# A gated trunk layer with three token mixers: a value head computed in the idle half of the key tile, longer modulation dots, and the norm's scale kept in PSUM

## The chip, the cores and the metric

The kernel runs on one core of one Trainium2 chip. The metric is the time of one execution in microseconds of device time. Three runs of the kernel before the change took 1243.07 to 1245.12 us, median 1244.29.

## The reference

Two layers over 512 tokens of width 1024, in float32. What matters here, cut from the reference:

```python
mod = c_silu @ w_ada + b_ada                       # one vector per layer
shift, scale, gate = jnp.split(mod, 3, axis=-1)
u = rms_norm(x, norm_g) * (1 + scale[:, None]) + shift[:, None]
z = u @ w_in
(aq, ak, av, ag, iq, ik, iw, bq, bk, bv, bg, cq, ck, cv, cg, ma, mb, mc) = jnp.split(z, SPLIT_OFFSETS, axis=-1)
...
merged = (jax.nn.sigmoid(ma) * (ya @ w_br_a) + jax.nn.sigmoid(mb) * (yb @ w_br_b) + jax.nn.sigmoid(mc) * (yc @ w_br_c))
return x + gate[:, None] * (merged @ w_out)
```

ya, yb and yc are the outputs of a sparse attention with an indexer, a sliding-window attention with two key and value heads (bv has 128 columns, 64 per head), and a stick-breaking attention. The indexer has one key of 64 columns (ik), to which the rotary embedding is applied. After the second layer there is a last rms norm.

## The kernel before, in words

**Data.** Activations lie transposed: 128 features on the partitions, 512 tokens along the free axis, eight such tiles for a width of 1024. A float32 product is made of three matmuls: each operand is split into a rounded high part and a remainder (uh and ul for u, whi and wlo for a weight), and high x high, low x high and high x low are added up in PSUM. Weights arrive in chunks of 128 x 512 (tile wstage) and are split on ACT, DVE or POOL.

**Stages of a layer.** `first_phase` (L880) computes the seven tiles of `FIRST` (L57) k step by k step, as each u tile becomes ready: two gate tiles (cg0, cg1), two merge gates (mc0, mc1), the indexer's key (ik) and its queries (iq0, iq1). The key has 64 columns only, so its tile holds it twice. Seven accumulators take all three ps_z slots and four of the five ps_s slots. `v_phase` (L929) computes what is wanted with tokens on the partitions, the values and the indexer's weights: here u is the stationary operand, and 1156 weight columns (`VCOLS`) stream in three groups of 386, 386 and 384 (`VGRP`, L75), for 8 k steps and 4 token blocks each. Then come the three mixers, gates and branch products, interleaved, and `out_phase` (L1291), which adds the result to x, sums the squares for the next norm and, in the last layer, writes the result.

**Norm and modulation.** The sum of squares comes from a matmul with a matrix of -1 into a PSUM bank (`nbank`); `rstd_of` (L748) takes Ln and Exp on ACT, from PSUM into an SBUF tile `zs`. `make_u` (L752) multiplies x by the norm's gain times (1 + scale) (`amul`, one number per partition) and by rstd in one DVE instruction, adds the shift (ACT), rounds to uh and subtracts for ul. For the first two tiles shift and rounding are one step.

The modulation vector is a product of a vector with a matrix. It is computed on DVE as dots of a 128 x 512 piece of weights with the broadcast vector (`csr`), with an accumulator output; two pieces make one column of `mods`. In layer 0 the dots for shift and scale stand in the way of the first u tiles: `ada_load` (L706) and `ada_first` (L711), four pieces of 256 KB for each k step, staged in the slots of tiles yh and yl that the mixers use later. Their elementwise result goes to another tile (`junk`, L686). For the first k step some filler matmuls (`FILL`, L42) read the staged pieces. The dots of later modulations run in other stages, on other tiles.

**Rotary.** `rope_evac` (L791) copies the tile from PSUM to zs, moves 32-row blocks by four DMAs into m2, multiplies by cosine and sine tables and adds.

**Order of the work.** The functions only record instructions. `Weave` interleaves the stages' items, and `Recorder` (L244 on) then plans: each instruction has a modelled price (`price`, L304), may run on one of several engines where alternatives are given, and each tile class has a fixed number of slots (`SLOTS`, L150). `forward` (L372) schedules all instructions by these prices, five rounds with priorities taken from the round before, and the best round's order is emitted for each engine. In the model a DMA lands 1.9 us after its issue, or when the DMA before it has landed, plus its bytes over 290 GB/s (L316, L460). All engines run in order, so a changed price can move any instruction of the program. All instructions have line L536 in the profile, so groups go by tiles.

Of the kernel before, what the change touches and what calls it, by code (L numbers as in the profile page):

```python
# [25 lines left out]
F32 = mybir.dt.float32  # L26
F32R = mybir.dt.float32r
# [25 lines left out]
def _cols(name, lo, n):  # L53
# [7 lines left out]
    ("mc1", _cols("mc", 128, 128)),  # L61
    ("ik", _cols("ik", 0, 64) + _cols("ik", 0, 64)),
    ("iq0", _cols("iq", 0, 128)),
# [12 lines left out]
VOFF = (0, 386, 772)  # L76

# [44 lines left out]
def by_tile(wv, *gens):  # L122
# [6 lines left out]
    while live:  # L129
# [15 lines left out]
        else:  # L145
# [3 lines left out]

SLOTS = {"t": 14, "e": 2, "zs": 2, "m2": 2, "zc": 2, "G": 2, "sm": 2, "yh": 5, "yl": 5, "Q": 2, "KH": 2, "dot": 2, "dotg": 2,  # L150
         "m8": 2, "mx": 2, "nm": 2, "den": 2, "wstage": 4, "whi": 4, "wlo": 4, "ps_z": 3, "ps_s": 5}
# [92 lines left out]
class Recorder:  # L244
# [59 lines left out]
    def price(self, x, engine, op, args, kw):  # L304
# [254 lines left out]
def trunk(ctx, tc, xT, vecs, w_ss, w_gt, w_first, w_t, w_v, w_br, w_o, rope, consts, out):  # L559
# [125 lines left out]

    def junk(l, m, w):  # L686
        if l == 0 and m < 16:
            return t512("t", 10) if m % 8 < 2 else t512("e", 2)
        return w

    def dot(l, m, q, w, o):
        DVE.scalar_tensor_tensor(junk(l, m, w), w, 1.0, csr[:, S * (q % 2):S * (q % 2) + S], op0=OP.mult, op1=OP.mult, accum_out=o[:, q:q + 1])
        if q % 2:
            DVE.tensor_scalar(mods[l][:, m:m + 1], o[:, q - 1:q], o[:, q:q + 1], b_ada[l][:, m:m + 1], op0=OP.add, op1=OP.add)
# [11 lines left out]
    def ada_load(j):  # L706
        st["wada", j] = [t512(t, 5) for t in ("yh", "yl", "yh", "yl")]
        for q in range(4):
            SP.dma_start(st["wada", j][q], w_ss[0, j, q])

    def ada_first(j):  # L711
        for q in range(4):
            if j < 2:
                for _ in range(FILL[4 * j + q]):
                    mm(st["nbank" if j else "warm"][:, :P], f(nones), st["wada", j][q][:, :P], not j)
            ada_step(0, j, q, st["wada", j][q])

# [22 lines left out]
    def rstd(cs_):  # L740
        if cs_.start == 0:
            st["nbank"], st["rstd"] = sbank(), t512("zs", 2)
        p, t = st["nbank"][:, cs_], st["rstd"][:, cs_]
        mm(p, f(nones), st["sq"][:, cs_], True, False)
        mm(p, f(nones), st["sq7"], False)
        rstd_of(p, t)

    def rstd_of(p, t):  # L748
        ACT.activation(t, p, AF.Ln, bias=epst, scale=-1.0 / D)
        ACT.activation(t, t, AF.Exp, scale=-0.5)  # L750

    def make_u(l, k, xk, cs_=FULL):  # L752
        t = t512("e", 2)[:, cs_]
        sh = mods[l][:, k:k + 1]
# [4 lines left out]
        uh, ul = st["uh"][k][:, cs_], st["ul"][k][:, cs_]  # L759
        if k < 2:  # L760
            if l == 0 and (k or cs_.start):
                ACT.activation(uh, t, AF.Identity, bias=sh)
            else:
                DVE.tensor_scalar(uh, t, sh, None, op0=OP.add)
            DVE.scalar_tensor_tensor(ul, t, sh, f(uh), op0=OP.add, op1=OP.subtract)
        else:
            ACT.activation(t, t, AF.Identity, bias=sh)
            cast(uh, t)
            both(ul, t, f(uh), OP.subtract)

# [63 lines left out]
    def evac(name, z):  # L834
        kind = name[:2] if name[2:] else name
        if kind in ("ag", "bg", "cg"):
            gate_evac(z, name)
        elif kind in ("ma", "mb", "mc"):
            m_evac(z, name)
        elif kind == "cq":  # L840
            st[name] = stack_q(z, 0.125, sbuf=False)
        elif kind == "ck":
            st[name] = stack_k(z, sbuf=False)
        elif kind in ("aq", "bq", "iq"):
            st[name] = stack_q(rope_evac(z))
# [34 lines left out]
    def first_phase(l):  # L880
# [29 lines left out]
        if l == 0:  # L910
            yield op(0, lambda: ada_load(3))
            yield op(0, lambda: ada_first(2))
        yield op(0, lambda: make_u(l, 2, st["x"][2]))
        yield op(9000, two if l else two0, *chunks(0), *chunks(1))
        for k in range(2, KT):
            if k + 1 < KT:
                if l == 0:
                    if k + 2 < KT:
                        yield op(0, lambda k=k: ada_load(k + 2))
                    yield op(0, lambda k=k: ada_first(k + 1))  # L920
                yield op(0, lambda k=k: make_u(l, k + 1, st["x"][k + 1]))

# [6 lines left out]
    def v_phase(l):  # L929
        def prep():  # L930
            st["vc"] = rec.tile("vc", [P, 4, S], F32)
            st["va"] = rec.tile("va", [P, 4, S], F32)
            st["vb"] = rec.tile("vb", [P, 4, P], F32)
            st["iw"] = rec.tile("iw", [P, 4, 4], F32)
        yield op(0, prep)
        dests = (("vc", 0, 512, 1.0), ("vb", 512, 640, 1.0), ("va", 640, 1152, 1.0), ("iw", 1152, 1156, 0.0625))
        for g in range(3):
# [353 lines left out]
    def out_phase(l):  # L1291
# [74 lines left out]
    def start():  # L1366
# [17 lines left out]
        x = st["x"] = [xx[k // 4][:, k % 4] for k in range(KT)]  # L1384
        nb = st["nbank"] = sbank()
        st["rstd"] = t512("zs", 2)

        def norm(cs_):
# [3 lines left out]
            for k in range(0, KT, 2):  # L1392
# [141 lines left out]
```

## Time and profile before

| | |
|---|---|
| median of three runs | 1244.29 us |
| the profiled execution | 1245.02 us |
| its span, first to last instruction | 1243.2 us |
| first tiles of layer 0, first to last matmul | 13.7 to 65.6 us |
| value stage of layer 0 | 65.6 to 116.1 us |
| first tiles of layer 1, value stage of layer 1 | 629 to 669 us, 669 to 716 us |
| last matmul of the output product | about 1233.5 us |

PE is TensorE, PEld its weight loads, DVE VectorE, ACT ScalarE, POOL GpSimd, and SP the engine that issues most DMAs. An instruction is named by its tiles, out<-in: `ps_z<-uh,whi` is a matmul into a PSUM tile of class ps_z. Ends of matmuls are modelled, so the spacing of starts, not the length of a row, tells the rate.

### The profile page before, as it was taken

The page shows a single profiled execution, that of the slowest core. Times are in us where ns is not written, and L with a number is a line of the kernel's source. Part 1 is how long each engine was busy: PE and PEld are TensorE (multiplying, and loading weights), DVE is VectorE, ACT ScalarE, POOL GpSimd, SP SyncE. Part 2 cuts the span into 40 slices and gives each one's busy share as a digit, 9 for nine tenths or more (in the row PEclk, how much of TensorE's full clock was granted, in tenths as well). Part 3 has the DMA queues.
Part 4 walks back from the last instruction along what each step waited for, and adds up shares of the span by engine and source line. Part 5 has one row for each costly group of instructions (what it writes and reads, how often), then busy time and mean ns, then how long its engine had stood idle before and what let it go on. Part 6 is the DMA issues. An engine that isn't in the chain of part 4 may idle for free.

```text
span 1243.2 us, 17837 instructions
## 1 busy us (share of the span) xinstructions
PE 1212.5 (98%) x5976; PEld 986.7 (79%) x5976; DVE 977.9 (79%) x2152; ACT 560.0 (45%) x1157; POOL 242.6 (20%) x274
## 2 busy tenths in 40 slices
PE   7899999999999999999999999999999999999997
PEld 5699777778877887778899987777787788877886
DVE  7966999999778877777476589999886888667654
ACT  4343677553255532642143157764533554244212
POOL 1010334532122111011200015343310211100120
PEclk9999999999999999999999999999999999999999
DMA  9644232324433455334633422223342233322243
GB/s 315 202 123 125 77 94 58 96 93 134 113 102 94 136 155 143 93 119 119 191 106 97 132 88 85 77 77 102 102 127 68 77 102 110 102 69 77 93 119 102
DMA packets 82012, 139.67 MB, mean 112 GB/s; under 512 B 10240, under 2 KB 22784, under 8 KB 81920
## 3 DMA queue, kind: packets, MB, share of 16 engines
q1 hardware_dynamic: 80768, 136.44, 36.8%
q10 hardware_dynamic: 1152, 2.10, 0.5%
q8 instruction: 47, 0.77, 0.3%
q14 instruction: 45, 0.37, 0.1%
HBM read 125.91 MB, written 4.19 MB: 105 GB/s over the span
## 4 chain that ended last, share of the span: by engine, by line
PE 80%; DVE 12%; ACT 3%; DMA 2%; issue 1%; SPq 1%; DVEq 0%; ACTq 0%
PE ps_z L536 58%; PE ps_s L536 22%; DVE t L536 4%; DVE Q L536 2%; SPq L536 1%; DVE m L536 1%; ACT t L536 1%; DVE e L536 1%; DVE score L536 1%; DVE vc L536 1%; DMA m<-zs 1%; DVE wstage L536 1%; DVE wlo L536 1%; DMA yl<-in_w_ss 0%; DMA wstage<-in_w_t 0%
## 5 line engine op out<-in xcount | busy, mean ns | idle before, releaser
L536 PE MATMUL ps_z<-uh,whi 128*128 128x512 f32 (+1 forms) x908 | 359.8, 398 | 7.6 <-ACT uh L536 4.9
L536 PE MATMUL ps_z<-ul,whi 128*128 128x512 f32 (+1 forms) x908 | 356.5, 393 | 0.0
L536 PE MATMUL ps_z<-uh,wlo 128*128 128x512 f32 (+1 forms) x908 | 355.4, 392 | 0.0
L536 POOL TENSOR_TENSOR wlo<-wstage,whi 128x512 fp32r<-128x512 f32 (+1 forms) x129 | 170.4, 1322 | 677.8 <-DVE whi L536 365.6
L536 PEld LDWEIGHTS ps_z<-uh,whi 128*128 128x128 f32 x908 | 170.8, 189 | 48.5 <-ACT uh L536 6.5
L536 PEld LDWEIGHTS ps_z<-uh,wlo 128*128 128x128 f32 x908 | 171.0, 188 | 38.5 <-issue 0.3
L536 PEld LDWEIGHTS ps_z<-ul,whi 128*128 128x128 f32 x908 | 171.3, 189 | 37.4 <-issue 2.6
L536 DVE CAST whi<-wstage 128x512 fp32r<-128x512 f32 (+2 forms) x181 | 76.3, 422 | 128.6 <-PE ps_z L536 109.8
L536 DVE TENSOR_TENSOR wlo<-wstage,whi 128x512 fp32r<-128x512 f32 (+2 forms) x243 | 159.2, 660 | 16.1 <-ACT whi L536 7.7
L536 ACT CAST whi<-wstage 128x512 fp32r<-128x512 f32 (+2 forms) x138 | 81.5, 596 | 168.1 <-PE ps_z L536 115.9
L536 ACT ACTIVATE e<-ps_z 128x512 f32<-128x512 f32 x68 | 40.3, 593 | 125.6 <-PE ps_z L536 125.4
L536 ACT ACTIVATE e<-e 128x512 f32<-128x512 f32 x96 | 60.3, 631 | 47.2 <-DVE e L536 46.3
L536 ACT ACTIVATE t<-t,nm 128x256 f32<-128x256 f32 (+3 forms) x128 | 65.1, 510 | 29.1 <-DVE nm L536 29.1
L536 ACT ACTIVATE t<-t 128x512 f32<-128x512 f32 x120 | 72.5, 628 | 7.3 <-DVE t L536 4.1
L536 PE MATMUL ps_z<-yh,wlo 128*128 128x512 f32 x192 | 75.8, 395 | 0.0
L536 PE MATMUL ps_z<-yl,whi 128*128 128x512 f32 x192 | 75.7, 394 | 0.0
L536 PE MATMUL ps_z<-yh,whi 128*128 128x512 f32 x192 | 75.7, 396 | 0.0
L536 PE MATMUL ps_s<-small,t 128*128 128x128 f32 x432 | 59.7, 276 | 4.8 <-ACT t L536 3.8
L536 PEld LDWEIGHTS ps_s<-small,t 128*128 128x128 f32 x432 | 49.4, 141 | 16.8 <-ACT t L536 6.0
L536 POOL CAST whi<-wstage 128x512 fp32r<-128x512 f32 (+1 forms) x53 | 33.3, 628 | 129.7 <-PE ps_z L536 98.4
L536 DVE MAX8 m<-score 128x8 f32<-128x256 f32 (+2 forms) x96 | 53.3, 555 | 1.4
L536 DVE SCALAR_TENSOR_TENSOR wstage<-wstage,csr 128x512 f32<-128x512 f32 x64 | 46.4, 725 | 7.4 <-DMA wstage<-in_w_ss 5.5
(202 smaller groups left out, 2164.5 us busy)
## 6 DMA issues: line engine op xcount, KB each, us to landing
wstage<-in_w_t SPq DMA_DIRECT2D x212, 256.0 KB, 2.7
m<-zs SPq DMA_DIRECT2D x128, 64.0 KB, 2.0
wstage<-in_w_gt SPq DMA_DIRECT2D x32, 256.0 KB, 2.6
wstage<-in_w_ss SPq DMA_DIRECT2D x32, 256.0 KB, 2.7
wstage<-in_w_o SPq DMA_DIRECT2D x32, 256.0 KB, 2.6
wstage<-in_w_v SPq DMA_DIRECT2D x32, 193.0 KB, 2.5
yh<-in_w_ss SPq DMA_DIRECT2D x16, 256.0 KB, 5.1
yl<-in_w_ss SPq DMA_DIRECT2D x16, 256.0 KB, 5.2
```

Of the source, the lines that this page charges most:

```text
L536: getattr(self.real[engine], y.op)(*[real(a) for a in y.args], **{k: real(v) for k, v in y.kw.items()})
```

## The change

Six things, in one diff:

1. The second half of the ik tile holds the 64 columns of the second value head of bv. `key_and_value` copies the tile to zs, builds the key's second half by a DMA, applies rotary, and brings the value half to tokens on the partitions by four transposes into a ps_s bank and a copy. The value stage then streams 1092 columns in three groups of 364.
2. The dots of layer 0 take 1024 columns each, staged in one class `Y` of 128 x 1024 tiles by DMAs of 512 KB, and overwrite their weights in place. The bias is added by a TENSOR_TENSOR.
3. rstd stays in PSUM: Ln and Exp write the bank of the sum of squares.
4. x is multiplied by rstd in place (`times_rstd`), on DVE, as soon as rstd is there.
5. `make_u` then computes scale and shift in one instruction, twice: once rounded (uh) and once not (t), each on ACT or DVE, and ul is their difference.
6. The planner's DMA rate is 365 GB/s instead of 290.

```diff
-    ("ik", _cols("ik", 0, 64) + _cols("ik", 0, 64)),
+    ("ik", _cols("ik", 0, 64) + _cols("bv", 64, 64)),
...
-VCOLS = _cols("cv", 0, 512) + _cols("bv", 0, 128) + _cols("av", 0, 512) + _cols("iw", 0, 4)
-VGRP = (386, 386, 384)
+VCOLS = _cols("cv", 0, 512) + _cols("bv", 0, 64) + _cols("av", 0, 512) + _cols("iw", 0, 4)
+VGRP = (364, 364, 364)
...
-            y.cost, y.lag, y.mode = 0.35 if engine == "SP" else 0.1, n * 4 / 290e3, "dma"
+            y.cost, y.lag, y.mode = 0.35 if engine == "SP" else 0.1, n * 4 / 365e3, "dma"
...
     def ada_load(j):
-        st["wada", j] = [t512(t, 5) for t in ("yh", "yl", "yh", "yl")]
-        for q in range(4):
-            SP.dma_start(st["wada", j][q], w_ss[0, j, q])
+        st["wada", j] = [rec.tile("Y", [P, 2 * S], F32) for _ in range(2)]
+        for i in range(2):
+            SP.dma_start(st["wada", j][i].rearrange("p (a b) -> p a b", a=2), w_ss[0, j, 2 * i:2 * i + 2].rearrange("q p s -> p q s"))
     def ada_first(j):
...
+        o = rec.tile("dot", [P, 4], F32)
+        for i in range(2):
+            w, m = st["wada", j][i], 8 * i + j
             if j < 2:
...
+                for q in range(2):
+                    for _ in range(FILL[4 * j + 2 * i + q]):
+                        mm(st["nbank" if j else "warm"][:, :P], f(nones), w[:, S * q:S * q + P], not j)
+            DVE.scalar_tensor_tensor(w, w, 1.0, csr, op0=OP.mult, op1=OP.mult, accum_out=o[:, i:i + 1])
+            DVE.tensor_tensor(out=mods[0][:, m:m + 1], in0=o[:, i:i + 1], in1=b_ada[0][:, m:m + 1], op=OP.add)
+        DVE.scalar_tensor_tensor(amul[0][:, j:j + 1], mods[0][:, 8 + j:9 + j], 1.0, g_sb[0][:, j:j + 1], op0=OP.add, op1=OP.mult)
...
+    def rstd_of(t):
+        ACT.activation(t, t, AF.Ln, bias=epst, scale=-1.0 / D)
         ACT.activation(t, t, AF.Exp, scale=-0.5)
+    def times_rstd(xk, cs_=FULL):
+        DVE.tensor_tensor(out=xk[:, cs_], in0=xk[:, cs_], in1=st["rstd"][:, cs_], op=OP.mult)
     def make_u(l, k, xk, cs_=FULL):
         t = t512("e", 2)[:, cs_]
-        DVE.scalar_tensor_tensor(t, xk[:, cs_], amul[l][:, k:k + 1], st["rstd"][:, cs_], op0=OP.mult, op1=OP.mult)
+        sc, sh = amul[l][:, k:k + 1], mods[l][:, k:k + 1]
...
+        for o in (st["uh"][k][:, cs_], t):
+            rec.add({"ACT": ("activation", (o, xk[:, cs_], AF.Identity), dict(scale=sc, bias=sh)),
+                     "DVE": ("tensor_scalar", (o, xk[:, cs_], sc, sh), dict(op0=OP.mult, op1=OP.add))})
+        both(st["ul"][k][:, cs_], t, f(st["uh"][k][:, cs_]), OP.subtract)
...
+    def key_and_value(z):
+        zs, m2, zc = t512("zs"), t512("m2"), t512("zc")
+        cast(zs, z)
+        cast(zc[H0], z[H0])
+        SP.dma_start(zc[H1], zs[H0])
+        for a, b in ((0, 32), (32, 0), (64, 32), (96, 0)):
+            SP.dma_start(m2[a:a + 32], zs[b:b + 32])
+        both(zc, zc, cos_t, OP.mult)
+        both(m2, m2, sin_t, OP.mult)
+        both(zc, zc, m2, OP.add)
+        tb = sbank()
+        for t in range(4):
+            PE.transpose(tb[:, 128 * t:128 * t + 128], zs[:, 128 * t:128 * t + 128], ident)
+        v = st["vb"] = rec.tile("vb", [P, 4, P], F32)
+        cast(v[:, :, 64:128], tb.rearrange("p (a b) -> p a b", a=4)[:, :, 64:128])
+        return zc
...
         if cs_.start == 0:
-            st["nbank"], st["rstd"] = sbank(), t512("zs", 2)
+            st["rstd"] = sbank()
```

In `start`, `first_phase` and `out_phase` the calls of `times_rstd` are added ahead of `make_u`; for the first two tiles of layer 0 they stand ahead of the dots. At the end of layer 1 the products with rstd now read PSUM.

More of the change, by code (lines that the diff above doesn't have):

```diff
@@ L146, in by_tile @@
             yield item
-SLOTS = {"t": 14, "e": 2, "zs": 2, "m2": 2, "zc": 2, "G": 2, "sm": 2, "yh": 5, "yl": 5, "Q": 2, "KH": 2, "dot": 2, "dotg": 2,
+SLOTS = {"t": 14, "e": 2, "zs": 2, "m2": 2, "zc": 2, "G": 2, "sm": 2, "Y": 5, "Q": 2, "KH": 2, "dot": 2, "dotg": 2,
          "m8": 2, "mx": 2, "nm": 2, "den": 2, "wstage": 4, "whi": 4, "wlo": 4, "ps_z": 3, "ps_s": 5}
@@ L684, in trunk @@
     amul = [fixed(f"amul{l}", [P, 8], F32) for l in range(L)]
[L686 to L689, printed above, removed]
     def dot(l, m, q, w, o):
-        DVE.scalar_tensor_tensor(junk(l, m, w), w, 1.0, csr[:, S * (q % 2):S * (q % 2) + S], op0=OP.mult, op1=OP.mult, accum_out=o[:, q:q + 1])
+        DVE.scalar_tensor_tensor(w, w, 1.0, csr[:, S * (q % 2):S * (q % 2) + S], op0=OP.mult, op1=OP.mult, accum_out=o[:, q:q + 1])
         if q % 2:
@@ L741, in rstd @@
         if cs_.start == 0:
-            st["nbank"], st["rstd"] = sbank(), t512("zs", 2)
-        p, t = st["nbank"][:, cs_], st["rstd"][:, cs_]
+            st["rstd"] = sbank()
+        p = st["rstd"][:, cs_]
         mm(p, f(nones), st["sq"][:, cs_], True, False)
         mm(p, f(nones), st["sq7"], False)
-        rstd_of(p, t)
-    def rstd_of(p, t):
-        ACT.activation(t, p, AF.Ln, bias=epst, scale=-1.0 / D)
+        rstd_of(p)
+    def rstd_of(t):
+        ACT.activation(t, t, AF.Ln, bias=epst, scale=-1.0 / D)
         ACT.activation(t, t, AF.Exp, scale=-0.5)
+    def times_rstd(xk, cs_=FULL):
+        DVE.tensor_tensor(out=xk[:, cs_], in0=xk[:, cs_], in1=st["rstd"][:, cs_], op=OP.mult)
     def make_u(l, k, xk, cs_=FULL):
         t = t512("e", 2)[:, cs_]
-        sh = mods[l][:, k:k + 1]
-        DVE.scalar_tensor_tensor(t, xk[:, cs_], amul[l][:, k:k + 1], st["rstd"][:, cs_], op0=OP.mult, op1=OP.mult)
+        sc, sh = amul[l][:, k:k + 1], mods[l][:, k:k + 1]
         if cs_.start == 0:
@@ L758, in make_u @@
             st["ul"][k] = t512(f"ul{k}", 1, F32R)
[L759 to L769, printed above, removed]
+        for o in (st["uh"][k][:, cs_], t):
+            rec.add({"ACT": ("activation", (o, xk[:, cs_], AF.Identity), dict(scale=sc, bias=sh)),
+                     "DVE": ("tensor_scalar", (o, xk[:, cs_], sc, sh), dict(op0=OP.mult, op1=OP.add))})
+        both(st["ul"][k][:, cs_], t, f(st["uh"][k][:, cs_]), OP.subtract)
     def sigmoid_from(z, s=None):
@@ L912, in first_phase, with next_u @@
             yield op(0, lambda: ada_first(2))
-        yield op(0, lambda: make_u(l, 2, st["x"][2]))
+        def next_u(k):
+            times_rstd(st["x"][k])
+            make_u(l, k, st["x"][k])
+        yield op(0, lambda: next_u(2))
         yield op(9000, two if l else two0, *chunks(0), *chunks(1))
@@ L932, in prep @@
             st["va"] = rec.tile("va", [P, 4, S], F32)
-            st["vb"] = rec.tile("vb", [P, 4, P], F32)
             st["iw"] = rec.tile("iw", [P, 4, 4], F32)
         yield op(0, prep)
-        dests = (("vc", 0, 512, 1.0), ("vb", 512, 640, 1.0), ("va", 640, 1152, 1.0), ("iw", 1152, 1156, 0.0625))
+        dests = (("vc", 0, 512, 1.0), ("vb", 512, 576, 1.0), ("va", 576, 1088, 1.0), ("iw", 1088, 1092, 0.0625))
         for g in range(3):
@@ L1017, in finish_pair @@
         DVE.tensor_tensor(out=t, in0=y, in1=st.pop(f"{b}g{p}"), op=OP.mult)
-        yh = t512("yh", 5, F32R)
-        yl = t512("yl", 5, F32R)
+        y2 = rec.tile("Y", [P, 2 * S], F32R)
+        yh, yl = y2[:, :S], y2[:, S:]
         cast(yh, t)
@@ L1384, in start @@
         x = st["x"] = [xx[k // 4][:, k % 4] for k in range(KT)]
-        nb = st["nbank"] = sbank()
-        st["rstd"] = t512("zs", 2)
+        nb = st["nbank"] = st["rstd"] = sbank()
         def norm(cs_):
@@ L1405, in norm @@
                 prev = t
-            rstd_of(nb[:, cs_], st["rstd"][:, cs_])
+            rstd_of(nb[:, cs_])
         norm(HALVES[0])
+        for k in (0, 1):
+            times_rstd(x[k], HALVES[0])
         ada_load(0)
@@ L1413, in start @@
         norm(HALVES[1])
+        for k in (0, 1):
+            times_rstd(x[k], HALVES[1])
         ada_load(1)
```

11 lines of the change are left out of this document (4 added, 7 removed).

## The prediction

> **What bounds the kernel now.** I read the busy times first. The numbers below are busy microseconds, share of the span and instruction count.
>
> ```profile
> span 1243.2 us, 17837 instructions
> PE 1212.5 (98%) x5976; PEld 986.7 (79%) x5976; DVE 977.9 (79%) x2152; ACT 560.0 (45%) x1157; POOL 242.6 (20%) x274
> ```
>
> TensorE (PE) is idle for 1243.2 - 1212.5 = 30.7 us. The kernel can become faster in two ways only: fewer matmul columns, or less of this idle time. So I asked next where the idle time is. The table by stretch gives, after the stretch and its length, the busy time (and count) of PE, weight load (PEld), DVE, ACT and POOL, then the granted clock, the DMA share and GB/s.
>
> ```profile
> 14.00:20.00 6.00, 3.71 (x24) 2.74 (x22) 5.86 (x19) 2.70 (x6) 0.00 (x0) 1.00 1.06 376
> 49.00:61.00 12.00, 10.66 (x44) 8.21 (x45) 11.28 (x30) 3.92 (x7) 0.30 (x1) 1.00 0.30 96
> 66.00:119.00 53.00, 53.00 (x303) 52.61 (x302) 34.52 (x77) 17.42 (x39) 2.19 (x3) 1.00 0.47 131
> 119.00:625.00 506.00, 501.66 (x2412) 397.80 (x2411) 414.18 (x919) 241.19 (x501) 118.05 (x129) 1.00 0.37 112
> 632.00:669.00 37.00, 37.00 (x196) 31.66 (x195) 25.39 (x50) 12.57 (x23) 0.00 (x0) 1.00 0.34 97
> ```
>
> Three limits show. From 14 to 61 us, the first tiles of layer 0, DVE is busy 5.86 of 6 and 11.28 of 12 us while PE waits: VectorE bounds the start. DMA reached 376 GB/s early on and fell to 96 later, so it does not bound the end of this stage. In the value stage (66 to 119) and in the first tiles of layer 1 (632 to 669) PE never stops. The attention and gate stage (119 to 625) has 4.3 us of PE idle in 506. So columns count fully in the value stage, DVE work counts in the start, and DVE work elsewhere has cover.
>
> What DVE does in the start, by group, from 12.7 to 61 us (count, then busy us and mean ns):
>
> ```profile
> L536 DVE SCALAR_TENSOR_TENSOR e<-yl,csr 128x512 f32<-128x512 f32 x12 | 8.2, 683 | 0.0
> L536 DVE SCALAR_TENSOR_TENSOR e<-yh,csr 128x512 f32<-128x512 f32 x12 | 8.2, 682 | 0.0
> L536 DVE TENSOR_TENSOR wlo<-wstage,whi 128x512 fp32r<-128x512 f32 x8 | 5.5, 684 | 0.0
> L536 DVE TENSOR_TENSOR wlo<-wstage,whi 128x384 fp32r<-128x384 f32 x8 | 4.4, 550 | 0.0
> L536 DVE TENSOR_SCALAR mods<-dot,small 128x1 f32<-128x1 f32 x14 | 3.8, 272 | 0.4
> ...
> L536 DVE SCALAR_TENSOR_TENSOR e<-va,amul,zs 128x512 f32<-128x512 f32 x4 | 3.0, 752 | 0.1
> ```
>
> The modulation dots are the largest item: two belong to each of the 14 mods, so 28 run in this stretch, 24 of them in the rows shown. The chain of waits shows how the last k step (one k step is one eighth of the contraction) gets from its dots to PE:
>
> ```profile
> 56.55 1.23 DVE e L536 x4
> ...
> 58.12 0.17 DVE amul L536
> ...
> 60.70 0.73 PE ps_z L536 x2
> ```
>
> Two dots and their accumulator reads take 1.23 us. From the end of amul (58.29) to the first matmul of k = 7 it is 2.41 us: the scaled product on DVE, the shift on ACT, the rounding to uh.
>
> **The change part by part.**
>
> Value stage. A matmul's spacing by width comes from unbroken pieces of the same chain: 386 columns, 512 columns, transposes, 256 columns.
>
> ```profile
> 65.75 17.36 PE ps_s L536 x98
> ...
> 382.18 16.62 PE ps_z L536 x72
> ...
> 398.81 2.18 PE ps_s L536 x20
> ...
> 624.33 5.55 PE ps_z L536 x47
> ```
>
> 17.36/98 = 0.177, 16.62/72 = 0.231, 5.55/47 = 0.118 us: 0.43 ns per column above 386, 0.45 below, so 0.44. Each group has 8 x 4 x 3 = 96 matmuls, and the groups lose 22, 22 and 20 columns: 96 x 64 x 0.44 = 2.70 us per layer, **-5.4 us** (5.2 to 5.6).
>
> [...]
>
> Transposes. Four per layer at 2.18/20 = 0.109 us are 0.87 us, with the change of mode before and after I take **+1.1 us** (0.9 to 2.0 if PE must also wait for zs). Copying the value half out of PSUM is one pass over 256 columns, on ACT or DVE, which have 35.6 and 18.5 us free in 66 to 119. The extra copy and the fifth DMA of the indexer key go on queues whose result is first needed by the indexer after 116 us, where the value stage ends, and the value chunks queued behind that DMA on SP have a DMA share of 0.47 in this stretch: no charge.
>
> PSUM banks. Five slots serve ps_s. Before, the sum of squares left its slot early and the value stage's first bank took it. Now rstd keeps the slot to the last k step and the bank of the transposes takes it next, so the value matmuls wait until an evacuation frees one of the first tiles' banks. The timelines at both ends of the first tiles:
>
> ```profile
> 65.59 0.34 PE L536 MATMUL ps_s<-wlo,uh 128*128 128x386 f32 x1
> ...
> 65.86 0.68 DVE L536 TENSOR_TENSOR zc<-ps_s,rt 128x512 f32<-128x512 f32 x1
> ...
> 66.31 0.58 ACT L536 ACTIVATE e<-ps_s 128x512 f32<-128x512 f32 x1
> ```
>
> ```profile
> 668.98 0.58 ACT L536 ACTIVATE e<-ps_s 128x512 f32<-128x512 f32 x1
> 669.03 0.40 PE L536 MATMUL ps_z<-uh,wlo 128*128 128x512 f32 x1
> 669.27 0.34 PE L536 MATMUL ps_s<-whi,uh 128*128 128x386 f32 x1
> ```
>
> In layer 0 the value matmuls are wanted at 65.59 and the first bank frees at 65.86 + 0.68 = 66.54; in layer 1 at 669.27 and 668.98 + 0.58 = 669.56. That is 0.95 + 0.29 = 1.24 us, and the planner can put the evacuations earlier or the transposes into the gap: **+1.0 us** (0 to 3).
>
> DVE in the start, over the seven k steps j = 1 to 7. A column costs (684 - 550)/128 = 1.05 ns. A pair of 512-column dots takes 1.23 us; one 1024-column dot keeps one fixed part: 1.23/2 + 0.512 x 1.05 = 1.15. Saved: 14 x 0.08 = 1.1 us. The add of the bias: 0.272 for a TENSOR_SCALAR with two per-partition operands, about 0.17 (as amul, also 128 x 1) for the TENSOR_TENSOR: 14 x 0.10 = 1.4. The product with rstd without a per-partition operand: 0.684 for 0.752, six times, and four half-width ones taken alike: 0.7. Together -3.2 us. The two outputs uh and t take the place of the shift and the rounding, on ACT, which has 8.1 of 12 us free, or DVE: no charge (bound: two uh on DVE more, +0.9).
>
> Multiplying by rstd from PSUM: zc<-ps_s,rt takes 0.68 us from PSUM, wlo 0.684 from SBUF, so no charge. [...]
>
> The chain of the last k step gets shorter: x times rstd is ready before the dots, and after amul there is one TENSOR_SCALAR or ACTIVATE. From 2.41 us I leave 0.55 (the 0.43 us of such a pass and the hand-over), and the 0.61 us of the product now lies ahead of the dots: -1.2 us.
>
> Against it: in the start, filler matmuls read the staged weights, and the dot now overwrites them in place, where before it wrote elsewhere. So it must wait for the fillers, and what is queued behind it on DVE waits too: the bias adds, amul and uh of k = 0, for which PE waits.
>
> ```profile
> 11.28 1.06 PE L536 MATMUL ps_s<-yl,nones 128*128 128x128 f32 x8
> 13.73 0.36 PE L536 MATMUL ps_z<-uh,whi 128*128 128x256 f32 x1 [1.39 <-DVE uh L536]
> ```
>
> The fillers end at 12.34. A 1024-column dot from there, its read, two short operations and uh (1.15 + 0.1 + 0.35 + 0.4) put the first matmul at about 14.4 instead of 13.73. **+0.7 us** (0 to 1.5). The start comes to -3.2 - 1.2 + 0.7 = **-3.7 us**. Its ends: -0.8, with the bounds for uh and the fillers and no shorter chain; and -7, three quarters of what PE idles (3.6 us in the 18 us shown, so some 9.5 in the 47 from 14 to 61). PE could follow: a k step costs it 21 x 0.231 = 4.85 us and takes 5.7 now (44 matmuls in 12 us).
>
> Nothing for three places. In layer 1's first tiles DVE has 11.6 of 37 us free under a PE that never stops; one more short pass at its beginning is hidden, and so is the wait of the product, which overwrites x, for the store of that x tile. The load of modulation weights in 512 KB pieces moves the same bytes. At the end the products with rstd can no longer go to POOL, but they did not:
>
> ```profile
> 1236.71 2.77 DVE L536 TENSOR_TENSOR t<-xm,zs 128x256 f32<-128x256 f32 x8 [1.45 <-ACT zs L536]
> ```
>
> [...]
>
> Sum: -5.4 + 1.1 + 1.0 - 3.7 = **-7.0 us**. The profiled execution took 1245.0 us (span 1243.2), and the runs have a median of 1244.3: 1237.3 us against the median. 0.2%, about what a measurement of this kernel can tell from no change, is 2.5 us.
>
> **The rivals.**
>
> The start gains nothing. The planner's order may give DVE both outputs, or the waits at the fillers hold more behind them than I count. For it: DVE stays the bound by any count, and its savings are made of tenths. Against: every replaced instruction has a cheaper row. Then only -5.4 + 1.1 + 1.0 = -3.3 remains, 1241.0 us; with a longer wait for banks it is within 0.2%.
>
> Weight loads bound the value stage. Then narrower groups save nothing, and the sum is 1.1 + 1.0 - 3.7 = -1.6, 1242.7 us. Against it is the 0.118 us spacing. [...]
>
> Slower: chunks arrive later than the planner now believes. It orders the queues of all engines by modelled times, and the change raises its DMA rate from 290 to 365 GB/s: a 256 KB chunk is modelled to land after 1.9 + 0.72 = 2.62 us, before after 1.9 + 0.90 = 2.80.
>
> ```profile
> wstage<-in_w_t SPq DMA_DIRECT2D x212, 256.0 KB, 2.7
> ```
>
> Measured is 2.7, so the old model was 0.1 us on the safe side and the new one is 0.08 late. Over 212 such chunks, and as many late splits in queues that run in order, all on PE's path, this is +17 us: 1237.3 + 17 = 1254. It decides for slower from 9.5 us, about 120 chunks. Against it: chunks are loaded four ahead, PE waits for none of them now, and at 376 GB/s in the busy start 256 KB take 0.70 us, near the new 0.72.
>
> **How the numbers follow.** The forecast has 0.58, the start without gain 0.24, the weight loads 0.04, slower by late chunks 0.08; 0.06 is left for a larger gain, where the planner finds more of PE's idle time in the start. With all terms at their better ends (-5.6, +0.9, 0, -7) the time is 1232.6, with all at their worse ends (-5.2, +2.0, +3, -0.8) 1243.3, which holds the second and third cases as well. I take 1232 to 1243. Faster by over 0.2%: the forecast and the larger gain, 0.64, nearly all but a tenth of the second case, 0.13, together 0.77. Same: what is left of the second, and the third, 0.15. Slower: 0.08.
>
> **What would show it.** Value groups at 0.167 us a matmul, about 48 us per layer for 288; eight 0.11 us transposes; DVE groups of sixteen 1024-column dots at about 1.2 us; the first k = 7 matmul near 57 and the value stage begun near 62 us; first matmul after 14 us; no loss in 632 to 669 or in the last 10 us. The forecast is wrong if PE idles more in 119 to 625 (new order), if the value stage starts with a gap over 2 us, or if k steps still take 5.7 us.

## The result, and the profile after

The changed kernel took 1233.21 us (median of six runs, 1232.74 to 1236.8) against 1243.84 us for the kernel before on the same chip (six runs, 1242.77 to 1245.12). The ratio is 0.9923, with a 95% interval of 0.9907 to 0.9938. The forecast was 1237.3 us, with a range of 1232 to 1243. The profiled execution took 1232.83 us, its span is 1231.0 us, 12.2 us shorter than the one before.

The busy times of the changed kernel, from its page:

```profile
span 1231.0 us, 17835 instructions
PE 1201.3 (98%) x5984; PEld 980.3 (80%) x5984; DVE 976.0 (79%) x2128; ACT 559.5 (45%) x1157; POOL 258.2 (21%) x278
```

PE's idle time is 29.7 us, nearly the 30.7 us of before. So the 12 us came out of PE's busy time, and the value groups, counted at 5.4 us, cannot be all of it.

The stages of the changed kernel, in the table by stretch (busy us and count of PE, PEld, DVE, ACT, POOL, then granted clock, DMA share, GB/s):

```profile
17.40:27.60 10.20, 7.85 (x30) 6.84 (x29) 8.25 (x21) 2.88 (x6) 1.74 (x1) 0.50 1.06 380
30.00:45.00 15.00, 15.00 (x83) 12.97 (x83) 14.43 (x27) 5.97 (x10) 3.97 (x4) 1.00 0.67 213
49.00:61.00 12.00, 10.46 (x44) 7.66 (x43) 11.65 (x24) 3.67 (x7) 2.04 (x2) 1.00 0.44 151
66.90:116.50 49.60, 48.32 (x289) 47.91 (x290) 31.04 (x67) 14.46 (x34) 1.88 (x3) 1.00 0.48 129
116.60:624.70 508.10, 503.01 (x2461) 401.43 (x2460) 420.38 (x939) 245.03 (x513) 121.49 (x126) 1.00 0.39 113
665.20:713.20 48.00, 48.00 (x291) 48.00 (x290) 31.11 (x67) 14.27 (x33) 3.16 (x5) 1.00 0.48 131
713.40:1223.40 510.00, 504.27 (x2465) 402.26 (x2463) 406.79 (x873) 240.98 (x503) 113.53 (x121) 1.00 0.33 93
```

The same view of the kernel before, for three stretches that were not shown:

```profile
30.00:45.00 15.00, 12.36 (x53) 9.30 (x53) 14.71 (x40) 7.34 (x13) 1.79 (x3) 1.00 0.84 256
116.20:629.00 512.80, 508.46 (x2461) 404.34 (x2460) 420.64 (x936) 244.74 (x509) 118.05 (x129) 1.00 0.38 112
720.00:1235.30 515.30, 509.31 (x2464) 404.58 (x2463) 407.41 (x871) 240.11 (x503) 111.71 (x123) 1.00 0.31 92
```

"Middle" below means the stretch of mixers, gates and output that follows a value stage. In layer 0 it runs up to the first tiles of layer 1. It became 4.7 us shorter in layer 0 and 5.3 us in layer 1, with the same matmuls and, but for the product with rstd at its end, without an edit in it. Four places of PE's timeline in the changed kernel show the rest (start, length, instruction, and in brackets the idle time before it and who ended it):

```profile
15.98 0.50 PE L536 MATMUL ps_z<-uh,whi 128*128 128x256 f32 x2 [3.71 <-ACT uh L536]
...
60.65 0.74 PE L536 MATMUL ps_z<-uh,whi 128*128 128x512 f32 x2 [1.06 <-ACT uh L536]
...
65.59 0.66 PE L536 MATMUL ps_s<-small,zs 128*128 128x128 f32 x4
66.88 0.41 PE L536 MATMUL ps_s<-whi,uh 128*128 128x364 f32 x1 [0.63 <-DVE zc L536]
...
79.08 0.43 PE L536 MATMUL ps_s<-wlo,uh 128*128 128x364 f32 x1 [1.28 <-DVE wlo L536]
...
664.79 0.66 PE L536 MATMUL ps_s<-small,zs 128*128 128x128 f32 x4
665.20 0.41 PE L536 MATMUL ps_s<-whi,uh 128*128 128x364 f32 x1
```

The last k step of layer 0 begins at 60.65 us, before at 60.70, and what follows the first tiles begins at 65.59 us in both kernels: the start gained nothing. The difference of 12.2 us is made up like this, in us (minus is shorter):

| place | forecast | measured |
|---|---|---|
| up to the end of layer 0's first tiles | -3.7 | 0.0 |
| transposes, layers 0 and 1 | +1.1 | +0.66, +0.41 |
| wait for a PSUM bank, layers 0 and 1 | +1.0 | +0.63, 0 |
| value stage, layer 0 (50.64 to 49.71) | -2.7 | -0.9 |
| value stage, layer 1 (50.74 to 48.16) | -2.7 | -2.6 |
| middle, layers 0 and 1 | 0 | -4.7, -5.3 |
| rest | 0 | -0.4 |

### The profile page after: what moved, and what is told of

It reads as the page before. It is cut to its first block, busy times and chain, and to the rows that moved or that the text cites. A ratio compares the mean times of both kernels' runs of the same rounds, so it can differ in the third digit from the quotient of the medians.

```text
span 1231.0 us, 17835 instructions
## 1 busy us (share of the span) xinstructions
PE 1201.3 (98%) x5984; PEld 980.3 (80%) x5984; DVE 976.0 (79%) x2128; ACT 559.5 (45%) x1157; POOL 258.2 (21%) x278
## 4 chain that ended last, share of the span: by engine, by line
PE 79%; DVE 12%; ACT 3%; DMA 2%; issue 2%; SPq 1%; POOL 1%; DVEq 0%; ACTq 0%; POOLq 0%
PE ps_z L536 59%; PE ps_s L536 20%; DVE t L536 3%; ACT t L536 2%; DVE m L536 1%; DVE Q L536 1%; DVE score L536 1%; DMA wstage<-in_w_t 1%; DVE wstage L536 1%; SPq L536 1%; DVE Y L536 1%; DVE vc L536 1%; DVE e L536 1%; DMA vc<-in_xT 1%; DVE zc L536 0%
## 5 line engine op out<-in xcount | busy, mean ns | idle before, releaser
L536 POOL TENSOR_TENSOR wlo<-wstage,whi 128x512 fp32r<-128x512 f32 (+1 forms) x148 | 197.9, 1338 | 701.8 <-DVE whi L536 322.9
L536 ACT CAST whi<-wstage 128x512 fp32r<-128x512 f32 (+2 forms) x153 | 90.8, 596 | 212.9 <-PE ps_z L536 147.5
L536 DVE CAST whi<-wstage 128x512 fp32r<-128x512 f32 (+2 forms) x169 | 69.8, 413 | 124.3 <-PE ps_z L536 104.9
L536 DVE TENSOR_TENSOR wlo<-wstage,whi 128x512 fp32r<-128x512 f32 (+2 forms) x224 | 147.3, 661 | 18.0 <-ACT whi L536 9.2
L536 PE MATMUL ps_z<-Y,whi 128*128 128x512 f32 x384 | 121.6, 396 | 0.2
L536 PEld LDWEIGHTS ps_z<-Y,whi 128*128 128x128 f32 x384 | 71.6, 188 | 17.1 <-DVE xm L536 0.7
L536 PE MATMUL ps_z<-Y,wlo 128*128 128x512 f32 x192 | 76.0, 396 | 0.0
## 6 DMA issues: line engine op xcount, KB each, us to landing
Y<-in_w_ss SPq DMA_DIRECT2D x16, 512.0 KB, 6.4
```

The source lines that it names most:

```text
L536: getattr(self.real[engine], y.op)(*[real(a) for a in y.args], **{k: real(v) for k, v in y.kw.items()})
```

## The experiments

Two questions were open: why the middle became 10 us shorter, and why the start gained nothing. For the middle the first theory was that a new order is cheaper, either through the planner's DMA rate (theory) or through the value head (rival). All runs of a batch stand against the kernel before on the same chip, which took 1244.4 us (medians of 7, 7 and 13 runs: 1244.37, 1244.36, 1244.41).

### One part alone, one part undone

b_rate365 is the kernel before with one line changed; a_rate290 is the changed kernel with that line undone:

```diff
-            y.cost, y.lag, y.mode = 0.35 if engine == "SP" else 0.1, n * 4 / 290e3, "dma"
+            y.cost, y.lag, y.mode = 0.35 if engine == "SP" else 0.1, n * 4 / 365e3, "dma"
```

> The kernel before with one number changed: the planner's DMA rate, 365 for 290. Theory 1 (the gain between the stages of tiles, 4.7 us in layer 0 and 5.3 us in layer 1, comes from the new plan, and the new plan from the new rate): 1235 to 1239 us, and the half-width matmuls with vb take 1 us or more less per layer. Theory 2 (the gain comes from the value head that moved to the key's tile, which frees the value stage and shifts everything behind it): 1243 to 1245 us, the matmuls with vb as before.

> The changed kernel with the old DMA rate, 290, in the planner. Theory 1 (rate): the gain in the attention stages goes, 1239 to 1242 us. Theory 2 (value head): it stays, 1232 to 1234 us.

b_head is the kernel before with point 1 of the change alone: the tile table, `VCOLS`, `VGRP` and `key_and_value`.

```diff
-    ("ik", _cols("ik", 0, 64) + _cols("ik", 0, 64)),
+    ("ik", _cols("ik", 0, 64) + _cols("bv", 64, 64)),
...
-VGRP = (386, 386, 384)
+VGRP = (364, 364, 364)
...
-            r = rope_evac(z)
+            r = key_and_value(z)
```

> The kernel before with the value head alone (key tile, groups of 364, four transposes); modulation dots, norm and rate as before. Theory 1: the value groups give 2.7 us per layer less about 1 us for transposes and bank waits, 1239.5 to 1241.5 us. Theory 2 (the value head also brings the gain in the attention stages): 1231 to 1235 us.

b_mod is the kernel before with points 2 to 5 alone (dots, rstd in PSUM, scale and shift in one step). Its diff is the one of the change without the lines of b_head and of the rate.

> The kernel before with the modulation, norm and in-place dots of the change (points 2 to 5), without the value head and with the old DMA rate. Theory now: VectorE's savings are real but the start gives them back (fillers that hold the in-place dots, TensorE idle early and then at half clock), so the value stage begins between 65.5 and 68 us as before or later, its matmuls stay at 0.177, and only the order in the middle moves the time: 1237 to 1243. Rival, the prediction's: the start alone gains 3.7, the value stage begins near 62, 1240 with an unchanged middle.

Measured: b_rate365 1237.45 us (ratio 0.9946, 0.9931 to 0.9961), b_head 1237.29 us (0.9948, 0.9931 to 0.9965), b_mod 1244.13 us (1.0001, 0.9992 to 1.0011), a_rate290 1235.62 us (0.9935, 0.992 to 0.995). A changed number in the planner's model, which edits no instruction, is worth as much as the value head. Undone in the changed kernel it costs 2.4 us by the medians, with intervals that overlap, and not 7. So the gains do not add. The modulation part alone, four of the six points, is worth nothing. Only b_rate365 fell where a theory had put it; b_head and a_rate290 lie between the ranges of their two theories, and b_mod is a little slower than its range. Both theories of the middle fell short; what the runs have in common is that the planner ends up with another order.

### What the order changes: half-width matmuls

In the products of weights and values (`ps_s<-t,va`, `t,vb`, `t,vc`) each matmul uses 64 columns of the array, one of two heads. PE's timeline of the kernel before shows these matmuls at two rates:

```profile
254.79 1.73 PE L536 MATMUL ps_s<-t,vb 128*64 128x256 f32 x8
...
329.14 1.74 PE L536 MATMUL ps_s<-t,vb 128*64 128x256 f32 x16
```

Sixteen take as long as eight, 1.74 and 1.73 us. Where the planner happens to put a matmul of one head behind one of the other, the two start 0.01 us apart and run side by side, one pair every 0.22 us. Where it puts a head behind itself, each takes 0.22 us.

b_pair is the kernel before with one rule for the planner: the first head's matmul may start only when the second's can too, so that the second can follow directly on it.

```diff
                     mm(y[64 * e:64 * e + 64, 128 * j:128 * j + W], st["v" + b][:, j, c:c + 64], PT[bk][:, c0:c0 + W], j == 0)
+                rec.pair()
...
+    def pair(self):
+        x, y = self.list[-2:]
+        for j in y.preds.values():
+            if j is not x and j.i not in x.preds:
+                x.preds[j.i] = j
+                j.succs.append(x)
+        y.preds[x.i] = x
+        x.succs.append(y)
```

> The kernel before; in all weighted value products the planner must take the two heads' half-width matmuls (64 columns of the array each) one behind the other, since the first may start only when both can. Theory 1a (what the new plan gained is that more of these neighbours run side by side on the two halves of the array, 0.217 us for two instead of 0.43): the matmuls with vb fall from 9.9 to about 6.5 us per layer and the kernel to 1236 to 1239 us. Rival (order of heads is a mere symptom, the array gains nothing): 1243 to 1246 us, slower if the first of a pair now waits for the second one's operand.

Measured: 1219.6 us (1218.7 to 1220.92), ratio 0.9804 (0.9789 to 0.9819), 24.8 us faster and three times or more of what was expected. PE's timeline of b_pair, for the same products:

```profile
254.39 1.73 PE L545 MATMUL ps_s<-t,vb 128*64 128x256 f32 x16
```

And of the changed kernel, where nothing forces the order:

```profile
250.59 2.65 PE L536 MATMUL ps_s<-t,vb 128*64 128x256 f32 x16
...
326.70 1.73 PE L536 MATMUL ps_s<-t,vb 128*64 128x256 f32 x16
```

A layer has 96 such pairs. Counted by starts less than 0.05 us apart, 40 and 39 of them run side by side in the two layers of the kernel before, 51 and 50 in the changed kernel, 86 and 89 in b_pair. The changed kernel got part of this by chance. The same rule was then put on four more kernels: the changed one (a_pair), the changed one with the old rate (a_pair290), b_head (b_head_pair) and b_mod (b_mod_pair), each with the lines of b_pair.

> The changed kernel, with the two heads' half-width matmuls made neighbours in all products of weights and values. Theory: what the change gained in the middle stages is a part of what b_pair gained there by other means, and the value head and the start's share stand beside it: 1208 to 1214. Rival: the order that b_pair's plan happened on is worth more than the pairs themselves (these measured some 10 us per layer), and the changed kernel with pairs gets the pairs alone: 1217 to 1224.

> The kernel before with the value head alone and with the heads' half-width matmuls as neighbours. Theory: value head (2.2 to 2.6 per layer) and pairs lie in different stages and add to b_pair's 1219.6: 1213 to 1217. Rival: what b_pair won beyond its pairs (some 5 us) was its order, and this kernel's order has other waits for Q and t in the middle, as a_pair's had: 1220 to 1230.

> The changed kernel with pairs and the old DMA rate of the planner. Theory: the wait for Q near 236 us and for t near 275 us, and the half-clock windows after them, differ from plan to plan by 1 to 4 us per layer; half-width matmuls are the same as in a_pair (9.2 to 9.9 and 6.7 per layer), so the time lies in 1214 to 1232 and its distance to a_pair's 1229.5 is read from those waits. Rival: the rate of 365 is what spoils a_pair's order, and this one reaches 1214 to 1219.

> b_mod with pairs. Theory: half-width matmuls at 9.2 to 9.9 and 6.7 per layer, start at 65.5 to 68, value stage as before: 1218 to 1230, by the waits for Q and t. Rival: without value head and rate the order of b_pair is kept and it stands within 2 us of 1219.6.

Measured: a_pair 1229.49 us (0.9883, 0.9868 to 0.9897), b_head_pair 1220.4 (0.9817, 0.98 to 0.9833), a_pair290 1218.5 (0.9802, 0.978 to 0.9824), b_mod_pair 1219.53 (0.9808, 0.9794 to 0.9823). With pairs, the value head, the modulation part and both together change nothing that can be told from b_pair, and the new rate costs 11 us. The theory that the value head adds to the pairs fell, and a_pair came out slower than both of its ranges.

What sets the middle can be counted from the profiled executions. "Half-width" is the time from the start of each half-width matmul to the start of the next matmul, summed over the layer's 192. "Idle" is PE's idle time. "Half clock" is how long the granted clock stood at 0.5. All but the median are of one execution for each kernel, and how much half clock falls into one differs between equal executions (see the last section). All in us, layer 0 and layer 1:

| kernel | median | middle | idle | half-width | half clock |
|---|---|---|---|---|---|
| before | 1244.4 | 512.8, 515.3 | 4.3, 6.0 | 36.3, 36.3 | 3.4, 3.4 |
| after | 1233.2 | 508.1, 510.0 | 5.1, 5.7 | 33.2, 33.7 | 0, 0 |
| b_rate365 | 1237.5 | 507.8, 511.1 | 2.9, 4.4 | 34.5, 35.3 | 0, 0 |
| b_head | 1237.3 | 508.5, 512.0 | 3.4, 4.8 | 34.7, 34.7 | 0, 3.4 |
| b_mod | 1244.1 | 512.8, 513.7 | 5.4, 5.9 | 35.3, 35.2 | 3.4, 3.4 |
| a_rate290 | 1235.6 | 509.5, 512.8 | 2.9, 5.1 | 34.7, 34.7 | 3.4, 3.4 |
| b_pair | 1219.6 | 500.4, 500.3 | 5.2, 5.2 | 26.6, 25.2 | 0, 0 |
| a_pair290 | 1218.5 | 500.9, 503.3 | 4.8, 5.7 | 25.2, 25.2 | 3.4, 3.4 |
| a_pair | 1229.5 | 506.9, 506.7 | 8.3, 8.8 | 25.7, 25.7 | 10.2, 3.4 |

Take idle, half-width and 0.47 of half clock from each middle: what is left lies between 468.0 and 471.4 us in these and in the five kernels not listed, while the middles themselves differ by 15 us. (0.47 is from the kernel before: eight 512-column matmuls at 0.43 instead of 0.23 us in the 3.4 us from 280.68 us are 1.6 us.) So these three terms account for the differences, to within 3.4 us. For the change, half-width, half clock and idle read -3.1, -1.6 and +0.8 us in layer 0, and -2.6, -1.6 and -0.3 in layer 1, together 8.4 of the 10.0 us. For b_pair the half-width matmuls alone are 20.8 us.

The idle term is mostly two waits. One is for t on ACT, 1.9 us at 274 and 2.0 us at 871 us in the changed kernel. The other is for the rotated Q ahead of the first indexer or stick-breaking scores. The waits of PE from 225 to 245 us, in b_pair (us in total, times, longest):

```profile
PE ps_s L545 <- DVE Q L545: 1.6, 1, 1.6
```

and in a_pair:

```profile
PE ps_s L545 <- DVE Q L545: 3.7, 1, 3.7
```

a_pair waits 2.1 us longer here, and in the wait its clock falls to half: from 238.00 to 243.00 us its table by stretch shows 0.50:

```profile
234.00:238.00 4.00, 0.35 (x2) 0.00 (x0) 3.81 (x9) 1.50 (x3) 0.00 (x0) 0.79 0.00 0
238.00:243.00 5.00, 4.91 (x20) 4.65 (x21) 4.78 (x21) 0.75 (x2) 0.25 (x1) 0.50 0.34 65
```

VectorE is busy 3.81 of the 4 us in which PE waits: a faster PE only meets VectorE's Q earlier. Which wait each plan leaves was not predicted for any of them.

### Why the start gained nothing

Three causes were in question: GpSimd, which now works beside VectorE; the fillers that hold the in-place dots; and the clock. DVE and POOL in the timeline of the changed kernel, 11 to 34 us:

```profile
11.74 1.27 POOL L536 TENSOR_TENSOR wlo<-wstage,whi 128x512 fp32r<-128x512 f32 x1 [6.44 <-DVE whi L536]
...
12.30 1.79 DVE L536 SCALAR_TENSOR_TENSOR Y<-Y,csr 128x1024 f32<-128x1024 f32 x1
...
29.84 1.22 DVE L536 SCALAR_TENSOR_TENSOR Y<-Y,csr 128x1024 f32<-128x1024 f32 x1
...
31.60 1.31 POOL L536 TENSOR_TENSOR wlo<-wstage,whi 128x512 fp32r<-128x512 f32 x1 [12.46 <-PE ps_z L536]
...
31.66 2.33 DVE L536 SCALAR_TENSOR_TENSOR Y<-Y,csr 128x1024 f32<-128x1024 f32 x1
```

A dot takes 1.22 us alone, and these two took 1.79 and 2.33 us beside a wlo piece on GpSimd. A third, at 17.05 us, took 1.22 beside a piece that took 1.98 itself, so not every dot beside a piece is stretched. a_nopool keeps the steps that may run on VectorE or GpSimd, the wlo pieces among them, on VectorE in layer 0's first tiles (`early` is set at the start and taken back behind them):

```diff
-        rec.add({"DVE": how} if in_psum(a, b) else {"POOL": how, "DVE": how})
+        rec.add({"DVE": how} if in_psum(a, b) or st.get("early") else {"POOL": how, "DVE": how})
```

> The changed kernel, with the pieces of wlo and the other two-way steps of layer 0's first stage allowed to VectorE alone (no GpSimd there). Theory: GpSimd's steps that lie at the same time as VectorE's stretch those (1.22 to 1.79 and 2.33, 0.16 to 0.84, 0.54 to 1.52, some 4 us in all); without them the dots take 1.22 and k=7 begins 1 to 4 us earlier than 60.65, 1229 to 1232. Rival: VectorE then carries the wlo steps itself (8 of about 1 us) and the start stays or is later, 1233 to 1238.

a_junk lets the two dots of the first k step, whose weights the fillers read, write to a spare tile (not the first dot of each pair, as the expectation says), so that no filler holds them:

```diff
-            DVE.scalar_tensor_tensor(w, w, 1.0, csr, op0=OP.mult, op1=OP.mult, accum_out=o[:, i:i + 1])
+            DVE.scalar_tensor_tensor(w if j else rec.tile("KH", [P, 2 * S], F32), w, 1.0, csr, op0=OP.mult, op1=OP.mult, accum_out=o[:, i:i + 1])
```

> The changed kernel, with the product of the first dot of each pair written to a spare tile, so that the filler matmuls that read Y hold it no longer. Theory: the first real matmul (15.98) begins 1.5 to 2.3 us earlier, near 14, as before the change; if the half-clock window of 17.4 to 27.6 hangs on the idle time ahead of it, that goes too and k=7 begins 2 to 4 us earlier, 1229 to 1231. Rival: k=7 waits for the late chunks and the weights either way, 60 to 61, 1232 to 1234.

a_all has both and the pairs:

> The changed kernel with the three edits of a_nopool, a_junk and a_pair together. Theory: they bear on different stages and add, 1204 to 1212. Rival: the plan made anew takes back some of it and it stands where a_pair stands, within 2 us.

Measured: a_nopool 1239.02 us (0.9957, 0.9942 to 0.9972), a_junk 1233.47 (0.9917, 0.9898 to 0.9936), a_all 1225.93 (0.9853, 0.9838 to 0.9868). Neither cause alone holds the start: a_nopool is slower than the changed kernel, a_junk is not faster, and a_all, which lies between its two ranges, is no better at the start. The dots in a_all, by group, and its first waits of PE:

```profile
L545 DVE SCALAR_TENSOR_TENSOR Y<-Y,csr 128x1024 f32<-128x1024 f32 x14 | 17.1, 1219 | 0.0
```

```profile
15.35 0.50 PE L545 MATMUL ps_z<-uh,whi 128*128 128x256 f32 x2 [0.54 <-ACT uh L545]
...
22.12 0.79 PE L545 MATMUL ps_z<-uh,wlo 128*128 128x256 f32 x2 [4.73 <-DVE wlo L545]
```

Without GpSimd's pieces every dot of a_all takes 1.22 us, but the wlo pieces now queue behind the dots on VectorE, and PE waits 4.73 us for one. In a_junk the first matmul comes at 14.51 us, as its theory said, and then PE waits for a wlo on VectorE too:

```profile
14.51 0.51 PE L536 MATMUL ps_z<-uh,whi 128*128 128x256 f32 x2
...
23.14 0.80 PE L536 MATMUL ps_s<-uh,wlo 128*128 128x256 f32 x2 [6.12 <-DVE wlo L536]
```

What all kernels with the modulation part share is seen only by laying them side by side. In the nine of them, the changed one among them, the first matmul comes at 14.5 to 17.3 us and the clock stands at half for 10.2 to 13.7 us ahead of 30 us. In the five without it the first matmul comes at 13.3 to 14.8 us, and the clock stands at half for 0, 0, 0, 3.4 and 6.8 us. The fillers that keep PE busy there read the modulation weights, and these now arrive in pieces twice as large. In b_mod, without fillers to run, PE idles early:

```profile
9.87 1.07 PE L536 MATMUL ps_s<-Y,nones 128*128 128x128 f32 x4 [2.33 <-DMA Y<-in_w_ss]
...
17.11 0.80 PE L536 MATMUL ps_z<-uh,whi 128*128 128x256 f32 x2 [2.45 <-ACT uh L536]
...
24.99 0.77 PE L536 MATMUL ps_z<-uh,whi 128*128 128x256 f32 x2 [3.71 <-DVE uh L536]
```

In the kernel before the fillers began at 8.14 us, after a wait of 1.62 us for their weights, and waited 0.20 us more at 9.50; in the changed one they began at 8.86, after 1.11 us. That the piece size is the cause is argued, not shown: neither the old pieces with the new dots, nor fillers that read something else, were tried.

Nor does the end of the start hang on this early loss in the changed kernel. PE makes it good: from 48.70 us on each k step begins 0.87 us after its uh begins on ACT, and at 60.65 PE waits 1.06 us for uh again. What sets uh is VectorE, which ends the product that this last uh reads at 59.47 us, and VectorE's work did not become less. The table by stretch from 12.7 us to the start of the last uh, before and after:

```profile
12.70:60.22 47.52, 38.44 (x198) 30.86 (x198) 43.75 (x118) 19.01 (x35) 2.09 (x4) 1.00 0.77 254
12.70:59.78 47.08, 40.78 (x197) 33.93 (x197) 43.82 (x94) 17.78 (x31) 8.93 (x9) 0.89 0.76 257
```

VectorE's own steps became cheaper, and from 12.7 to 61 us it splits 11 wlo pieces instead of 17, with four on GpSimd. But it took over the second output of `make_u` (t, a tile of class e) in eight of ten cases, a new step on it; before, ACT added the shift for the six full tiles. From the changed kernel's groups, 12.7 to 61 us:

```profile
L536 DVE TENSOR_SCALAR e<-va,amul,mods 128x512 f32<-128x512 f32 x4 | 3.2, 789 | 0.0
...
L536 DVE TENSOR_SCALAR e<-vc,amul,mods 128x512 f32<-128x512 f32 x2 | 1.1, 543 | 0.0
L536 DVE TENSOR_SCALAR e<-vc,amul,mods 128x256 f32<-128x256 f32 x2 | 0.8, 406 | 0.0
```

By the spacing of starts these are 4.5 us. Steps beside GpSimd's pieces took some 4 us more than alone: two dots 1.7, one of these outputs 1.0 (1.52 us at 53.32), one ul 0.6, one bias add 0.7. In all fourteen kernels VectorE is busy for 41.8 to 44.8 us from 12.7 us to the last uh, and that uh begins at 59.8 to 63.0 us. No run keeps t on ACT, so its share is read from the rows and not tested; and in a_junk, where VectorE is busy for the least, 41.8 us, it idles the more, 5.5 us, and the last uh begins at 60.01.

As to the whole time, a_all beats a_pair by 3.6 us, but not in the start: its middles are 1.3 and 2.7 us shorter.

The best version is one with pairs. a_pair290, the changed kernel with the old rate, b_mod_pair, b_pair and b_head_pair cannot be told apart at 1218.5 to 1220.4 us.

## Why the prediction was right, and where it was wrong

**The value stage: right.** Nine matmuls of 364 columns in the chain of the changed kernel:

```profile
85.19 1.50 PE ps_z L536 x9
```

That is 0.167 us each, as worked out, and layer 1 gained 2.6 us for 2.7 predicted. PEld is busy 48.00 of 48.00 us in layer 1's value stage, and the matmuls are faster all the same; so the rival of the weight loads is out. No share of the load shows in the spacing at these widths: each column is worth 0.43 to 0.45 ns from 256 over 364 and 386 to 512 columns (0.118, 0.167, 0.177 and 0.231 us).

**Transposes and banks: right in kind and size.** 1.07 us for 1.1, and 0.63 us for 1.0. In layer 1 the bank came in time. The 0.2 us that the prediction added for a change of mode can be compared with one thing in the trace: the first value matmul behind the transposes takes 0.24 us (66.88 to 67.12) and 0.25 us (665.20 to 665.45) where the ones after it take 0.167. In the kernel before, without transposes, the first one takes 0.18 us like the others. That a change of mode is the cause was not shown.

**"No charge" for the extra copy and DMA of the key: wrong, +1.3 us in layer 0.** The row at 79.08 shows the wait. The timelines of VectorE and of SP's DMA issues show its cause. Before:

```profile
67.95 1.03 SPq L536 DMA_DIRECT2D wstage<-in_w_v  x2
...
69.38 0.69 DVE L536 TENSOR_TENSOR m<-m,rt 128x512 f32<-128x512 f32 x1 [0.91 <-DMA m<-zs]
...
77.66 0.55 DVE L536 TENSOR_TENSOR wlo<-wstage,whi 128x386 fp32r<-128x386 f32 x1
```

After:

```profile
66.06 0.67 DVE L536 COPY zc<-ps_s 64x512 f32<-64x512 f32 x1
...
68.75 1.03 SPq L536 DMA_DIRECT2D wstage<-in_w_v  x2
...
70.18 0.69 DVE L536 TENSOR_TENSOR m<-m,rt 128x512 f32<-128x512 f32 x1 [0.87 <-DMA m<-zs]
...
78.49 0.53 DVE L536 TENSOR_TENSOR wlo<-wstage,whi 128x364 fp32r<-128x364 f32 x1
```

The copy (0.67 us) and the DMA push the rotary steps on both queues 0.8 us back, and the wlo piece behind them from 77.66 to 78.49. Besides, that piece belongs to the sixth weight chunk of the stage, where before it was the seventh: one chunk fewer is split ahead of the rotary steps, and PE wants it 12 matmuls sooner. How the two share the 1.3 us stays open. That it comes with the value head is shown: PE waits 0.5 to 1.7 us for a wlo between 69 and 116 us in all nine kernels with the head, and 0.3 us at most in the five without. The cover that I named, free time of DVE over the whole stage, was there; the queue at that place was not free. With transposes and banks the value head is worth 1.8 us in its own stages, not 3.3.

**"The start -3.7": wrong, 0.0.** Each replaced step did become cheaper: from the first dot of a k step's second column to amul it is 1.46 us (51.17 to 52.63), before 1.65 (50.29 to 51.94). The bias add fell to 0.16, and the product that reads PSUM takes 0.68 us, as in the group of VectorE's instructions from 12.7 to 61 us in the changed kernel:

```profile
L536 DVE TENSOR_TENSOR va<-va,ps_s 128x512 f32<-128x512 f32 x4 | 2.6, 681 | 0.0
```

The PSUM operand costs nothing that shows: 681 ns with it, 684 for a TENSOR_TENSOR of the same size with both operands in SBUF (wlo, in the kernel before).

The step that failed is "no charge" for the two outputs uh and t, with 0.9 us as its bound. VectorE got t eight times, 4.5 us, and together with the steps that GpSimd stretched this took back all that the cheaper steps and the wlo pieces given away had saved (43.75 and 43.82 us busy). The sign that the prediction named for this is there: 44 matmuls from 49 to 61 us in both kernels, so k steps take as long as before. A second step failed too, but costs nothing at the end: the first matmul "at about 14.4". The dot began at 12.30, as reckoned from the fillers, but took 1.79 us beside GpSimd, and uh on ACT stood behind the rounding of a weight chunk that waited 2.90 us for its transfer. The first matmul came at 15.98, and after that idle time the clock stood at 0.50 from 17.4 to 27.6 us, which the prediction did not think of. From 30 to 45 us PE then does not wait at all (15.00 busy of 15 us, 12.36 before) and makes this good. The rival "the start gains nothing" is what happened, and by one of the means that it named in part: the planner gave VectorE most of one output, not of both.

**"The middle 0": wrong, -10.0 us.** The prediction had said that a changed price can move any instruction, and named new order only as a loss. It had taken PE's 4.3 us of idle time as all that the middle could give, since columns count fully. But the time of a column depends on its neighbour: 36 us per layer of half-width matmuls could be 25.

So the forecast of 1237.3 lay within 4.1 us, and the measured time within the range, by luck: the gain was counted 3.7 too high at the start, 1.5 too high in the value head's own stages and 10.0 too low in the middle, and these partly cancelled. Of the terms, only the value stage, the transposes and the banks came by the mechanism that was named.

## What to carry to other kernels

Where a planner orders all queues, an edit's own cost is only part of its effect: change one number of the planner that edits no instruction, and the spread of the times is the noise under every other change (here the medians moved by 6.9, 2.4 and 11.0 us in three kernels). Matmuls that use half of the array's columns belong next to a matmul for the other half (here 16 took 1.73 us side by side, and 8 as long one behind the other); look for equal rows with different counts in the timeline, and write the order down instead of leaving it to chance. A short step that is moved onto a queue is not free because the engine has time in that stage; look at what stands behind it in those few microseconds.

## What was unexpected of the hardware

**After a short wait the clock stood at half for 3.4 us, or not at all.** In the kernel before, in the table by stretch:

```profile
277.00:280.70 3.70, 2.00 (x15) 1.49 (x14) 3.67 (x9) 3.36 (x8) 1.89 (x2) 1.00 0.21 72
280.70:284.10 3.40, 3.40 (x9) 2.62 (x9) 3.37 (x8) 2.55 (x5) 0.00 (x0) 0.50 0.48 154
```

1.7 us of idle time in the piece before are followed by 3.4 us at 0.50, which costs 1.6 us. In the changed kernel a wait of 1.92 us, which ends at 274.43, is not:

```profile
269.95:273.36 3.41, 2.56 (x12) 1.72 (x10) 3.38 (x7) 3.08 (x13) 1.53 (x2) 1.00 0.00 0
273.36:276.78 3.42, 2.23 (x12) 1.65 (x13) 3.35 (x14) 2.94 (x10) 0.00 (x0) 1.00 0.40 112
275.70:280.00 4.30, 4.27 (x22) 3.60 (x23) 4.26 (x11) 3.86 (x10) 2.94 (x3) 1.00 0.37 108
```

Ahead of the last matmuls the clock stood at half for 3.41 us twice in the kernel before (280.68 to 284.10 and 884.84 to 888.26), and once in the changed one, for 10.24 us (17.36 to 27.60). In these two traces every stretch of full or half clock that ends in a change is a whole multiple of 3.413 us long: 81, 1, 176, 1 and 103 of them in the kernel before, 3, 3 and 351 in the changed one. So I counted both executions in pieces of that length from one change of the clock. The wait in the changed kernel is cut in two by the border at 273.36 us: PE was busy for 75% and 65% of the two pieces shown. The wait in the kernel before fell into one piece, 277.27 to 280.68 us, of which PE was busy for 50%. Half clock also followed the pieces from 881.43 us in the kernel before and from 13.95 us in the changed one, with PE busy for 40% of each, but neither the one from 236.31 us in the kernel before, busy for 48%, nor the one from 235.82 us in the changed kernel, busy for 50%; the busy share alone does not decide it. So 1.7 us of idle time were followed by 3.4 us at half clock, and a wait of 1.92 us by none. That it depends on where the wait falls in these pieces is my reading of these numbers and was not tested. Equal executions differ too: the changed kernel's six took 1232.7 to 1233.6 us at a mean clock of 0.993 to 0.996, and 1236.6 and 1236.8 us at 0.988 and 0.990.
